# 2x2 average pooling: larger stores, one order of transfers, and each transfer split over two queues

## The chip, the cores and the metric

The kernel runs on one core of a Trainium2 chip. The metric is the device time of the execution in microseconds (us). The profiler gives, for one execution, the span from the first to the last instruction and the work inside it.

## What is computed

The input is a float32 tensor of 32 x 128 planes of 256 x 256 numbers. Each plane is averaged over windows of 2 x 2 that do not overlap, so the output has planes of 128 x 128.

```python
n, c, h, w = 32, 128, 256, 256       # kernel_size = 2, stride = 2
for i in range(h_out):
    for j in range(w_out):
        window = x[:, :, 2*i : 2*i + 2, 2*j : 2*j + 2]
        output[:, :, i, j] = np.mean(window, axis=(2, 3))
```

1073.74 MB are read and 268.44 MB are written.

## The kernel before

Two neighbouring input rows make one output row. The kernel takes such a pair, 512 numbers or 2 KB, as a *unit*; there are 32 x 128 x 128 of them, 4096 for each of the 128 partitions. A *piece* is a number of units per partition that are loaded, worked on and stored together. The units of one partition in a piece lie one behind the other in memory, so a piece of 32 units is a run of 64 KB per partition in the input and a run of 16 KB per partition in the output.

The loop runs over a plan: 126 pieces of 32 units, then two groups of smaller pieces, 16, 8 and 8 units, and 8, 8, 8, 4, 2, 1 and 1 units (lines 58 to 65). For each piece it does five things:

1. The sync queue loads the piece into `in_tile` (line 84). There are two such tiles of 64 KB per partition, so a load waits until the piece two before it has been read.
2. VectorE adds the second row of each pair to the first, in place (line 87; 256 numbers for each unit).
3. VectorE adds each even column to the odd one next to it and writes `col_sum` (line 96; 128 numbers for each unit). There are three such tiles.
4. ScalarE multiplies by 0.25, in place (line 108).
5. ScalarE's queue stores the result (line 110).

Loads and stores are thus two separate streams. All loads are issued by SyncE, all stores by ScalarE, and both run on the same transfer engines at the same time. The framework's scheduler places the waits; the order of the instructions on each engine is that of the loop.

Of the kernel before, what the change touches and what calls it, by code (L numbers as in the profile page):

```python
# [1 line left out]

# [4 lines left out]


@with_exitstack  # L10
def kernel(
    ctx: ExitStack,
    tc: tile.TileContext,
    x: bass.AP,
    kernel_size: bass.AP,
    stride: bass.AP,
    out: bass.AP,
):
    nc = tc.nc
    P = nc.NUM_PARTITIONS  # L20

    n, c, h, w = x.shape
    k = int(kernel_size)
    s = int(stride)
    h_out = (h - k) // s + 1
    w_out = (w - k) // s + 1
    R = n * c * h_out

    if k == s and 2 <= k <= 4 and R > 0 and R % P == 0:
        _nonoverlap_pool(ctx, tc, x, out, k, n, c, h, w, h_out, w_out)  # L30
    else:
        _generic_pool(ctx, tc, x, out, k, s, n, c, h, w, h_out, w_out)


def _nonoverlap_pool(ctx, tc, x, out, k, n, c, h, w, h_out, w_out):
    nc = tc.nc
    P = nc.NUM_PARTITIONS
    s = k
    R = n * c * h_out

    hv = h_out * s
    xs = x if hv == h else x[:, :, 0:hv, :]
    xv = xs.rearrange("n c (ho a) w -> (n c ho) (a w)", a=s)
    ov = out.rearrange("n c ho wo -> (n c ho) wo")
    assert xv.shape == (R, s * w) and ov.shape == (R, w_out)

    wu = w_out * s

    unit_bytes = s * w * 4
    G_MAIN = max(1, min(R // P, (64 * 1024) // unit_bytes))  # L50

    total_units = R // P
    nmain, rem_units = divmod(total_units, G_MAIN)
    plan: list[list[int]] = [[G_MAIN] for _ in range(nmain)]
    if rem_units:
        plan.append([rem_units])

    if G_MAIN % 32 == 0 and nmain >= 4 and rem_units == 0:
        u = G_MAIN // 32
        tail = [  # L60
            [16 * u, 8 * u, 8 * u],
            [8 * u, 8 * u, 8 * u, 4 * u, 2 * u, u, u],
        ]
        assert all(sum(t) == G_MAIN for t in tail)
        plan = plan[:-2] + tail

    sbuf = ctx.enter_context(tc.tile_pool(name="sbuf", bufs=2))

    inv = 1.0 / float(k * k)

    r0 = 0
    for parts in plan:
        in_tile = sbuf.tile([P, G_MAIN, s * w], mybir.dt.float32, name="in_tile")
        g0 = 0
        for g in parts:
            rows = P * g
            xt = xv[r0 : r0 + rows].rearrange("(p g) f -> p g f", p=P)
            ot = ov[r0 : r0 + rows].rearrange("(p g) f -> p g f", p=P)
            r0 += rows

            it = in_tile[:, g0 : g0 + g]
            g0 += g

            nc.sync.dma_start(out=it, in_=xt)

            for di in range(1, k):
                nc.vector.tensor_add(  # L87
                    out=it[:, :, 0:w],
                    in0=it[:, :, 0:w],
                    in1=it[:, :, di * w : (di + 1) * w],  # L90
                )

            col_sum = sbuf.tile(
                [P, G_MAIN, w_out], mybir.dt.float32, name="col_sum", bufs=3
            )
            nc.vector.tensor_add(  # L96
                out=col_sum[:, :g],
                in0=it[:, :, 0:wu:s],
                in1=it[:, :, 1 : wu + 1 : s],
            )  # L100
            for dj in range(2, k):
                nc.vector.tensor_add(
                    out=col_sum[:, :g],
                    in0=col_sum[:, :g],
                    in1=it[:, :, dj : wu + dj : s],
                )

            nc.scalar.mul(out=col_sum[:, :g], in_=col_sum[:, :g], mul=inv)  # L108

            nc.scalar.dma_start(out=ot, in_=col_sum[:, :g])  # L110
        assert g0 <= G_MAIN

    assert r0 == R, (r0, R)


def _generic_pool(ctx, tc, x, out, k, s, n, c, h, w, h_out, w_out):
    nc = tc.nc
    P = nc.NUM_PARTITIONS

    planes = n * c  # L120
    xp = x.rearrange("n c h w -> (n c) h w")
    op = out.rearrange("n c ho wo -> (n c) ho wo")

    if h_out <= 0 or w_out <= 0 or planes == 0:
        return

    max_in_bytes_per_part = 48 * 1024

    def rows_for(bi):
        return (bi - 1) * s + k  # L130

    BI = 1
    while BI < h_out and rows_for(BI + 1) * w * 4 <= max_in_bytes_per_part:
        BI += 1

    inv = 1.0 / float(k * k)

    pool = ctx.enter_context(tc.tile_pool(name="gen", bufs=2))

    for p0 in range(0, planes, P):  # L140
        pn = min(P, planes - p0)
        for i0 in range(0, h_out, BI):
            bi = min(BI, h_out - i0)
            rows_needed = rows_for(bi)

            in_t = pool.tile([P, rows_for(BI), w], mybir.dt.float32, name="g_in")
            nc.sync.dma_start(
                out=in_t[:pn, :rows_needed, :],
                in_=xp[p0 : p0 + pn, i0 * s : i0 * s + rows_needed, :],
            )  # L150

            acc = pool.tile([P, BI, w_out], mybir.dt.float32, name="g_acc")
            first = True
            for di in range(k):
                for dj in range(k):
                    src = in_t[
                        :pn,
                        di : di + (bi - 1) * s + 1 : s,
                        dj : dj + (w_out - 1) * s + 1 : s,
                    ]  # L160
                    if first:
                        nc.vector.tensor_copy(out=acc[:pn, :bi, :], in_=src)
                        first = False
                    else:
                        nc.vector.tensor_add(
                            out=acc[:pn, :bi, :], in0=acc[:pn, :bi, :], in1=src
                        )

            nc.scalar.mul(out=acc[:pn, :bi, :], in_=acc[:pn, :bi, :], mul=inv)

            nc.scalar.dma_start(
                out=op[p0 : p0 + pn, i0 : i0 + bi, :], in_=acc[:pn, :bi, :]
            )


# [1 line left out]
_INS = ['x', 'kernel_size', 'stride']  # L177
_OUTS = [((32, 128, 128, 128), 'float32')]
#: Inputs that are plain numbers.
_NUMBERS = {'kernel_size': 2, 'stride': 2}  # L180


# [26 lines left out]
```

## Time and profile before

| | |
|---|---|
| device time, median of 10 runs | 3106.39 us (3106.22 to 3106.78) |
| device time of the profiled execution | 3106.49 us |
| its span | 3104.7 us |
| row add, 32 units (line 87) | 126 times, 8692 ns each |
| column add, 32 units (line 96) | 126 times, 4425 ns each |
| scale, 32 units (line 108) | 126 times, 3616 ns each |
| store, from issue to landing, median of the full pieces | 31.6 us |
| load, from issue to landing, median of the full pieces | 35.1 us |
| VectorE waits for loads, in total | 1406.7 us |
| ScalarE waits for VectorE, in total | 2635.8 us |

The busy time of an engine is the time in which it works; its idle time costs nothing where another resource sets the end. A load's time from issue to landing contains the time in which it waits for the transfers ahead of it. The queue named q1 carries the loads and q10 the stores. A packet is one contiguous run that one transfer engine moves, or the small write with which the engine reports that its part is done; each transfer has one of these on each of 16 engines.

The beginning and the end of the span, as the timeline shows them: the first load is issued at 0.73 us and VectorE starts on it at 22.65 us. The last full piece reaches VectorE at 3043.20 us. The last store, of one unit, is issued at 3102.36 us and lands 1.5 us later.

### The profile page before, as it was taken

To read this page: it belongs to the slowest core of one execution; us is meant where nothing else is said; L and a number is where in the kernel's file an instruction comes from. 1 tells how busy PE (TensorE), PEld (TensorE's weight loads), DVE (VectorE), ACT (ScalarE), POOL (GpSimd) and SP (SyncE) were. 2 spreads that over 40 slices of the span, in tenths; PEclk is the share of its full clock that TensorE was granted. 3 is DMA by queue.
4 is the path that set the end of the run, shared out by engine and by line. 5 is a ranking of instruction groups with operands and counts; after the bars stand their busy time and mean duration, and the time that the engine had idled before them with its cause. 6 is when DMAs were issued, how large, how long until landed. Compare 5 with 4: busy or idle time off the path is not lost. (4 is left out here: it accounts for less than half of the span.)

```text
span 3104.7 us, 1126 instructions
## 1 busy us (share of the span) xinstructions
DVE 1681.3 (54%) x272; ACT 465.8 (15%) x137; POOL 0.2 (0%) x4
## 2 busy tenths in 40 slices
DVE  4555555555555555555555555555555555555556
ACT  1111111111111111111111111111111111111112
POOL 0000000000000000000000000000000000000000
DMA  9999999999999999999999999999999999999999
GB/s 418 437 439 425 436 439 425 436 438 426 436 439 426 435 439 430 431 439 434 428 438 435 427 438 437 426 437 437 426 437 437 427 435 438 428 435 437 428 435 396
DMA packets 39176, 1342.26 MB, mean 432 GB/s; under 512 B 4352, under 2 KB 4736, under 8 KB 5888
## 3 DMA queue, kind: packets, MB, share of 16 engines
q1 hardware_dynamic: 19584, 1073.75, 79.9%
q10 hardware_dynamic: 19584, 268.44, 20.2%
q14 instruction: 8, 0.07, 0.0%
HBM read 1073.74 MB, written 268.44 MB: 432 GB/s over the span
## 5 line engine op out<-in xcount | busy, mean ns | idle before, releaser
L87 DVE TENSOR_TENSOR in_tile<-in_tile 128x8192 f32<-128x8192 f32 (+4 forms) x136 | 1113.8, 8190 | 1406.8 <-DMA in_tile<-in_x_dram 1406.7
L108 ACT ACTIVATE col_sum<-col_sum 128x4096 f32<-128x4096 f32 (+4 forms) x136 | 464.5, 3415 | 2635.8 <-DVE col_sum L96 2635.8
L96 DVE TENSOR_TENSOR col_sum<-in_tile 128x4096 f32<-128x4096 f32 (+4 forms) x136 | 567.7, 4174 | 14.0 <-DMA out_dram<-col_sum 1.9
L108 ACT ACT_TABLE_LOAD x1 | 1.3, 1283 | 0.7 <-PEq L190 0.7
L190 POOL MEMSET const-bfloat16-1.0<- 128x1 bf16 x1 | 0.1, 101 | 0.0
L190 POOL MEMSET const-uint8-127<- 128x1 uint8 x1 | 0.1, 101 | 0.0
L190 POOL MEMSET const-float32-0.0<- 128x1 f32 x1 | 0.1, 98 | 0.2 <-issue 0.2
L190 POOL MEMSET const-float32-1.0<- 128x1 f32 x1 | 0.1, 98 | 0.0
## 6 DMA issues: line engine op xcount, KB each, us to landing
out_dram<-col_sum ACTq DMA_DIRECT2D x126, 2048.0 KB, 31.6
in_tile<-in_x_dram SPq DMA_DIRECT2D x5, 2048.0 KB, 27.5
in_tile<-in_x_dram SPq DMA_DIRECT2D x1, 4096.0 KB, 25.5
out_dram<-col_sum ACTq DMA_DIRECT2D x5, 512.0 KB, 12.0
in_tile<-in_x_dram SPq DMA_DIRECT2D x126, 35.1
out_dram<-col_sum ACTq DMA_DIRECT2D x1, 1024.0 KB, 12.8
in_tile<-in_x_dram SPq DMA_DIRECT2D x1, 1024.0 KB, 16.2
in_tile<-in_x_dram SPq DMA_DIRECT2D x1, 512.0 KB, 16.8
```

Source lines behind the costliest of these rows:

```text
L87: nc.vector.tensor_add(out=it[:, :, 0:w], in0=it[:, :, 0:w], in1=it[:, :, di * w : (di + 1) * w],)
L96: nc.vector.tensor_add(out=col_sum[:, :g], in0=it[:, :, 0:wu:s], in1=it[:, :, 1 : wu + 1 : s],)
L108: nc.scalar.mul(out=col_sum[:, :g], in_=col_sum[:, :g], mul=inv)
L190: nc = _bacc.Bacc("TRN2", target_bir_lowering=False, num_devices=1)
```

## The change

The changed kernel computes the same thing with the same three operations per piece, and differs in how the data is moved.

- **Groups.** 127 units make a group, loaded in four pieces of 31, 32, 32 and 32 units. There are 32 groups and a rest of 32 units. In memory the rows of a group lie 254 KB apart from partition to partition, and a piece is a run of 62 or 64 KB in it.
- **Stores.** The results of a whole group are collected in `res`, a tile of 158 units per partition, and stored in one transfer with a run of 63.5 KB per partition. Groups use it from unit 0 and from unit 31 in turn, so that the first piece of a group doesn't overlap the results of the group before, while the other pieces do.
- **Order.** The schedule is written by hand. The store of a group is issued after the first load of the next group and before its second load.
- **Split.** Every transfer is issued in two halves: the even partitions on SyncE's queue and the odd partitions on ScalarE's queue. ScalarE's own instructions and its transfers are in one program order.
- **Last piece of a group.** Its column add and scale are done in two steps, all but 8 units and then 8 units.
- **Tail.** The rest is loaded in two halves of 16 units. In ScalarE's program order these loads stand behind the scales of the last group. The last group's store follows them; then the two halves are worked on and stored in one transfer of 16 KB per partition.

```diff
+IN_UNITS = 32
+GROUP = 127
+FIRST = GROUP - 3 * IN_UNITS
+
+def _pool_2x2(ctx, tc, x, out, units):
...
+    in_pool = ctx.enter_context(tc.tile_pool(name="inp", bufs=2))
+    out_pool = ctx.enter_context(tc.tile_pool(name="outp", bufs=1))
+    res = out_pool.tile([P, GROUP + FIRST, w_out], f32, name="res")
...
+    def move(dst, src):
+        nc.sync.dma_start(out=dst[0::2], in_=src[0::2])
+        nc.scalar.dma_start(out=dst[1::2], in_=src[1::2])
+
+    def rows(it):
+        nc.vector.tensor_add(out=it[:, :, 0:w], in0=it[:, :, 0:w], in1=it[:, :, w:])
+
+    def cols(it, dst):
+        nc.vector.tensor_add(out=dst, in0=it[:, :, 0:w:2], in1=it[:, :, 1:w:2])
+
+    def scale(dst):
+        nc.scalar.mul(out=dst, in_=dst, mul=0.25)
+
+    groups, rest = divmod(units - 1, GROUP)
+    rest += 1
...
+    for k in range(groups):
...
+        base = 0 if k % 2 == 0 else FIRST
+        spans = [(FIRST + i * IN_UNITS, IN_UNITS) for i in range(3)]
+        if base == 0:
+            pieces = [(0, FIRST)] + spans
+        else:
+            pieces = [(3 * IN_UNITS, FIRST)] + [(a - FIRST, g) for a, g in spans]
+        jobs += [(xt[:, a : a + g], g, res[:, base + a : base + a + g]) for a, g in pieces]
+        stores.append((ot, res[:, base : base + GROUP]))
+
+    ctx.enter_context(tc.manual_schedule())
...
+    def load(j):
+        if j < len(jobs):
+            src, g, _ = jobs[j]
+            tiles[j] = new_in()[:, :g]
+            move(tiles[j], src)
+
+    load(0)
+    load(1)
+    for j, (_, g, dst) in enumerate(jobs):
+        it = tiles.pop(j)
+        rows(it)
+        if j % 4 < 3:
+            cols(it, dst)
+            load(j + 2)
+            scale(dst)
+        else:
+            for a, b in ((0, g - 8), (g - 8, g)):
+                cols(it[:, a:b], dst[:, a:b])
+                scale(dst[:, a:b])
+            if j + 1 < len(jobs):
+                move(*stores[j // 4])
+                load(j + 2)
...
+    it, tout = new_in(), new_in()
...
+    for a, b in cuts:
+        move(it[:, a:b], xt[:, a:b])
+    move(*stores[-1])
+    for a, b in cuts:
+        rows(it[:, a:b])
+        cols(it[:, a:b], to[:, a:b])
+        scale(to[:, a:b])
+    move(ot, to[:, :rest])
```

The function `_nonoverlap_pool` and its plan are removed. The general path for other sizes stays as it is and isn't used here.

## The prediction

> **What bounds the kernel now.** I read the page's head first, then the slices, then the transfer queues, then windows over single stages, and last the timeline. The page:
>
> ```profile
> span 3104.7 us, 1126 instructions
> DVE 1681.3 (54%) x272; ACT 465.8 (15%) x137; POOL 0.2 (0%) x4
> DMA  9999999999999999999999999999999999999999
> DMA packets 39176, 1342.26 MB, mean 432 GB/s; under 512 B 4352, under 2 KB 4736, under 8 KB 5888
> q1 hardware_dynamic: 19584, 1073.75, 79.9%
> q10 hardware_dynamic: 19584, 268.44, 20.2%
> ```
>
> VectorE is busy for half the span, ScalarE for a seventh; the transfer engines are busy in all 40 slices. Loads (q1) and stores (q10) share their time as 80 to 20, as they share the bytes: a stored byte costs what a loaded one does. So the span is bytes, plus a price per packet, plus the time in which no packet moves. The windows (length, busy time of each engine, clock, transfer share, GB/s) show where the last part lies:
>
> ```profile
> 66.69:3043.20 2976.51, 1613.42 (x247) 444.78 (x123) 0.00 (x0) 1.00 1.00 433
> 3086.00:3098.00 12.00, 8.63 (x7) 2.74 (x3) 0.00 (x0) 1.00 0.96 394
> 3098.00:3104.70 6.70, 2.16 (x6) 1.03 (x3) 0.00 (x0) 1.00 0.33 119
> ```
>
> The first runs from the third to the 126th piece: 123 pieces of 8.389 MB in and 2.097 MB out in 2976.51 us, 24.199 us a piece, 433.3 GB/s, share 1.00. No gap is left there; only the last 7 us are thin. One period of the timeline:
>
> ```profile
> 2994.84 8.69 DVE L87 TENSOR_TENSOR in_tile<-in_tile 128x8192 f32<-128x8192 f32 x1 [10.97 <-DMA in_tile<-in_x_dram]
> 3003.63 4.43 DVE L96 TENSOR_TENSOR col_sum<-in_tile 128x4096 f32<-128x4096 f32 x1
> 3008.08 0.33 SPq L84 DMA_DIRECT2D in_tile<-in_x_dram  x1
> 3008.09 3.62 ACT L108 ACTIVATE col_sum<-col_sum 128x4096 f32<-128x4096 f32 x1 [20.56 <-DVE col_sum L96]
> 3011.73 0.34 ACTq L110 DMA_DIRECT2D out_dram<-col_sum  x1
> ```
>
> VectorE idles 11 us of 24 for the load: compute has room.
>
> [...]
>
> **The price of a packet.** 10.486 MB at 435.2 GB/s are 24.094 us. The other 0.105 us of a piece are spread over 18 packets per engine (8 loads, 8 stores, 2 completion writes): 5.8 ns each. From above, two short windows of the transfer view (packets, MB, share), the first with loads alone, the others the last 6.7 us:
>
> ```profile
> q1 hardware_dynamic: 112, 7.34, 99.6%
> ...
> q10 hardware_dynamic: 650, 0.76, 31.8%
> q1 hardware_dynamic: 20, 0.03, 1.3%
> ```
>
> 112 packets took 99.6% of 16 x 17 us = 270.9 us, their bytes need 269.9: 9 ns each. 670 took 33.1% of 16 x 6.7 = 35.5 us for bytes worth 29.0: 9.6 ns each. I take 5.8, which the loop shows with two queues at work, and keep 9.5 as the other end.
>
> **The change part by part.**
>
> (a) Fewer, larger packets. Before: 39168/16 = 2448 per engine. After: 128 loads plus 2 tail loads, each 8 packets and 2 completion writes per engine, 1300; 33 stores likewise, 330; together 1630. Saved: 818 x 5.8 ns = 4.7 us (7.8 at 9.5 ns).
>
> (b) One order instead of two streams. Four loads, then the store of the group before placed behind the first load of the next. In the loop this costs nothing if the queues never run dry. Usual piece: the next-but-one load is issued 13.2 us after VectorE starts (8.79 + 4.43), while the load between takes 18.7 to 19.3 us: 5 us of cover. Last piece of a group: 8.79, 24 columns units 3.36 (between 2.29 and 4.43 of the two sizes seen), ScalarE on 24 units 2.76 (between 1.91 and 3.62), on 8 units 1.06, hand-overs 0.1: the store is issued at 16.1, and the load behind it on both queues 0.34 later. The 31-unit load in flight covers 18.7. A 64 KB store lands 1.5 us after its issue, 0.15 of it data, so 1.35 us pass before or after the data: about 1.2 us of cover remain. Taken as nothing; without that cover each 0.1 us costs 31 x 0.1 = 3 us. The odd half of every load now stands in ScalarE's queue before a scale and waits for the column add; behind it only that scale waits, which waits for the same add. VectorE's second column add of a group waits for the store that reads this half of `res`; that store is ahead in the same queues of the load that VectorE waits for anyway.
>
> (c) VectorE and ScalarE: 32 further short instructions each, from splitting the last piece; hidden under 11 us of idle per piece.
>
> (d) The end. Start: VectorE's first instruction comes at 22.65, its 8.389 MB are worth 19.28 and 9 packets 0.05, so 3.3 us are fixed. Until the last big load (number 127): 1065.35 MB in and 31 stores of 8.323 MB out, 1323.37 MB, 3040.8 us; 1590 packets, 9.2 us. VectorE starts on it at 3053.3. By then SyncE has issued the even halves of both tail loads (they wait for piece 126 alone), but their odd halves stand in ScalarE's queue behind all scales of piece 127, until 3053.3 + 16.1 = 3069.4. The even halves, 4.19 MB, keep the engines busy for 9.7 us; then nothing can be sent until about 3070.7: **a gap of 7.7 us**. Then the odd tail halves (4.19 MB) and SyncE's even half of the big store (4.16 MB) share the engines. Packets of two queues alternate (a store of before, worth 4.8 us, took 31.6 to land beside a load): four of 1.2 and four of 2.4 us bring the first tail half in at 3085.2, the second by 3090.0. VectorE needs 2 x (4.43 + 2.29) = 13.5 us from 3085.2: 3098.7; ScalarE 1.91: 3100.6. The big store has ended at 3099.6, so there is a second gap of 2.3 us. The last store, 2.097 MB, lands 1.35 + 4.85 us later, 3106.8; before, 0.8 us lay between the last landing (issue 3102.36 plus 1.5) and the end. Span 3107.6.
>
> Against the profiled 3104.7 that is +2.9 us: 4.7 saved in the loop, the rest and 2.9 more given back in the tail, where the kernel before breaks its last two pieces down to one unit and stores each at once. The profiled execution took 3106.49 with its span of 3104.7; the median is 3106.39. I add 2.9 to the median: **3109.3 us**, no change by the bound used here: 0.2% is 6.2 us, 3100.2 to 3112.6, about what a measurement can tell from no change.
>
> **Rivals.**
> 1. Faster. Two queues with equal large packets hide each other's packet price wholly: the loop showed 5.8 ns with two queues, a single queue 9. That would save 1630 x 5.8 ns = 9.5 us more: 3099.8. Against it: the price was still there with two queues always full. The tail gap doesn't close in this case.
> 2. Slower: stores alone are slower than stores among loads. Before, both queues are at work in every slice, so no window shows writes alone; after, some 19 us in every 96 are nothing but writes. Their 268.4 MB are worth 617 us; each per cent less rate costs 6.2 us. It decides from half a per cent (3.3 us beyond my forecast); at 3%, a guess, 3128. For it: nothing but the absence of evidence; against: the equal cost per byte in the page.
> 3. The cover of 1.2 us at the end of each group fails, because a queue that joins late waits longer for its first packet: 1 us short is 31 us, 3140.
> 4. The change doesn't do what it says:[...] loads and stores would take twice as long, about 6200 us.[...]
>
> A load's rows per partition now lie 254 KB apart, not 64. [...]the 64 KB of before ran at full rate. I count a loss there with rival 2.
>
> **How the numbers follow.** Forecast 0.64 (its own range 3104 to 3114), rival 1 0.10, rival 2 0.18, rival 3 0.05, rival 4 0.03. Faster by over 0.2%: most of rival 1 and a sliver of the forecast, 0.08. Slower: rivals 2 to 4 but for small losses, 0.24, plus 0.06 of the forecast, 0.30. Same: 0.62. The range runs from just above rival 1 to within rival 2, 3101 to 3126.
>
> **What would show it.** Packets near 26,080 of the two queues; VectorE's starts on the pieces of a group spaced 38.5 (the store lies between), 19.3, 19.3 and 18.7 us, 95.9 in sum; transfer share 1.00 in any window of the loop; then a stretch near 3063 to 3070 with share 0, a second of 2 us before the last store, and VectorE's first tail add near 3085. A group period of over 96.2 us speaks for rival 2 or 3 (which of them, the window over the store tells); under 95.7, for rival 1. A tail load whose odd half leaves before piece 127 is scaled would prove step (d) wrong.

## The result, and the profile after

| | before | after |
|---|---|---|
| device time, median | 3106.41 us (29 runs) | 3134.29 us (8 runs, 3131.95 to 3138.40) |
| ratio to before | | 1.0089 [1.0081, 1.0098] |
| device time of the profiled execution | 3106.49 us | 3131.95 us |
| its span | 3104.7 us | 3130.2 us |

The changed kernel is 0.9% slower, 25 us more than the forecast of 3109.3 and 8 us above the upper end of the range. The profiled execution is the lowest of the eight, so the sums below explain 3131.95 and leave 2.3 us of the median unexplained.

The page of the changed kernel, head and transfer queues:

```profile
span 3130.2 us, 1398 instructions
DVE 1681.7 (54%) x292; ACT 467.5 (15%) x163; POOL 0.2 (0%) x4
DMA  9999999999999999999999999999999999999998
DMA packets 26090, 1342.28 MB, mean 429 GB/s; under 512 B 5216, under 2 KB 5216, under 8 KB 5216
q10 hardware_dynamic: 13040, 671.10, 50.0%
q1 hardware_dynamic: 13040, 671.10, 49.7%
```

The bytes are the same, the packets are the 2 x 13040 = 26080 that the forecast counted, VectorE is as busy as before, and the transfer engines are busy in every slice. Still the span is 25.5 us longer. The slices cannot show where: a loss of 0.7 us in every 97 does not move a digit. One turn of the loop on the timeline (start, length, engine, line, what it does, and in brackets the idle time before it):

```profile
1047.81 8.69 DVE L69 TENSOR_TENSOR in_tile<-in_tile 128x8192 f32<-128x8192 f32 x1 [6.19 <-DMA in_tile<-in_x_dram]
1056.61 4.49 DVE L72 TENSOR_TENSOR res<-in_tile 128x3072 f32<-128x3072 f32 x2
1060.00 3.71 ACT L75 ACTIVATE res<-res 128x3072 f32<-128x3072 f32 x2 [14.18 <-DVE res L72]
1063.74 0.51 SPq L65 DMA_DIRECT2D out_dram<-res  x1
1064.35 56.36 SPq L65 DMA_DIRECT2D in_tile<-in_x_dram  x3
1066.57 8.42 DVE L69 TENSOR_TENSOR in_tile<-in_tile 128x7936 f32<-128x7936 f32 x1 [5.47 <-DMA in_tile<-in_x_dram]
...
1107.00 8.69 DVE L69 TENSOR_TENSOR in_tile<-in_tile 128x8192 f32<-128x8192 f32 x1 [27.68 <-DMA in_tile<-in_x_dram]
```

The last piece of a group starts at 1047.81 and its store is issued at 1063.74, 15.9 us later (forecast: 16.1). VectorE starts the next piece at 1066.57 and the one behind the store at 1107.00. That is 40.4 us, and a store with a load is worth 38.5. In the mean of 29 groups, the second to the thirtieth, VectorE's starts lie 39.69, 18.63, 19.47 and 18.79 us apart, 96.58 in sum (the *period* below), against 38.5, 19.3, 19.3, 18.7 and 95.9 in the forecast. The excess of 0.68 us in each of 31 groups is 21 us, and VectorE in fact starts on the last piece of the last group at 3074.22, forecast 3053.3.

Windows of the changed kernel (length, busy time of DVE, ACT and POOL, clock, transfer share, GB/s), first before a store, in it and over its end, then three in the tail:

```profile
194.00:197.00 3.00, 0.00 (x0) 0.57 (x1) 0.00 (x0) 1.00 0.92 389
198.00:212.00 14.00, 12.14 (x2) 1.25 (x1) 0.00 (x0) 1.00 1.03 446
210.00:220.00 10.00, 0.17 (x1) 3.51 (x1) 0.00 (x0) 1.00 1.05 418
3083.00:3092.00 9.00, 4.49 (x2) 3.71 (x2) 0.00 (x0) 1.00 0.35 120
3113.00:3123.00 10.00, 7.50 (x3) 3.82 (x2) 0.00 (x0) 1.00 0.53 228
3123.00:3130.20 7.20, 0.00 (x0) 0.00 (x0) 0.00 (x0) 1.00 0.69 291
```

The store itself runs at full rate (446 GB/s at a share of 1.03; a share over 1 is an effect of the window's edges: its 96 packets, six an engine of 2.40 us, are counted whole in 14 us). At its end, from 210 to 220, the share is 1.05 and the rate only 418: packets are under way, and take longer than their bytes are worth. That is one thing that the page's shares hide.

The records of single packets show it directly. They do not name a transfer engine, so they were joined into 16 chains in which each packet begins where the one before it ended, to a few ns; the 20,864 packets with data fall into 16 chains of 1304. Away from the turns a load packet of 64 KB takes 2418 ns and a store packet of 63.5 KB 2399 ns, almost without scatter.

The records of the kernel before hold other sizes too, and give the prices. A packet of 4 bytes (there are 16 for each transfer, the completion writes) takes 9 ns, one of 2 KB 84, of 16 KB 611, of 32 KB 1213 and of 64 KB 2418, in the median. From 2 to 64 KB that is 2334 ns for 62 KB, 27.20 GB/s on an engine and 435.2 on the 16, which is the rate that the forecast reckons with; about 9 ns of each packet are left. In the chains of the changed kernel a packet begins some 4 ns before the one ahead has ended (2414 ns lie between the starts of two load packets of 64 KB), so that about 5 ns of the 9 count.

In the changed kernel, mean time above the usual, by place in the store:

```
store packets 2 to 6 of 8   +1 ns
store packet 7              +4 ns
store packet 8            +422 ns
first load packet behind  +176 ns
```

With the small gaps between them the turn from storing to loading costs 0.614 us on an engine, 31 x 0.614 = 19.0 us, nearly the whole loss of the loop. The other part of the loss is in the tail:

```profile
3074.22 8.69 DVE L69 TENSOR_TENSOR in_tile<-in_tile 128x8192 f32<-128x8192 f32 x1 [6.20 <-DMA in_tile<-in_x_dram]
3083.01 4.49 DVE L72 TENSOR_TENSOR res<-in_tile 128x3072 f32<-128x3072 f32 x2
3086.40 2.76 ACT L75 ACTIVATE res<-res 128x3072 f32<-128x3072 f32 x1 [14.74 <-DVE res L72]
3087.60 1.13 ACTq L66 DMA_DIRECT2D in_tile<-in_x_dram  x2
3089.07 1.04 ACT L75 ACTIVATE res<-res 128x1024 f32<-128x1024 f32 x1
3090.14 0.51 SPq L65 DMA_DIRECT2D out_dram<-res  x1
...
3098.80 4.42 DVE L69 TENSOR_TENSOR in_tile<-in_tile 128x4096 f32<-128x4096 f32 x1 [11.29 <-DMA in_tile<-in_x_dram]
3111.58 2.29 DVE L72 TENSOR_TENSOR in_tile<-in_tile 128x2048 f32<-128x2048 f32 x1 [8.36 <-DMA in_tile<-in_x_dram]
...
3122.50 0.50 SPq L65 DMA_DIRECT2D out_dram<-in_tile  x1
```

The odd tail halves leave on ScalarE's queue only at 3087.60, when the last column add has ended (3083.01 + 4.49), and the window from 3083 shows the hole that this makes: a share of 0.35. From 3074.22 to the end are 56.0 us; the forecast had 54.3.

### The profile page after: what moved, and what is told of

The parts are those of the page before. It is cut to its first block, busy times and chain, and to the rows that moved or that the text cites. A ratio compares the mean times of both kernels' runs of the same rounds, so it can differ in the third digit from the quotient of the medians.

```text
span 3130.2 us, 1398 instructions
## 1 busy us (share of the span) xinstructions
DVE 1681.7 (54%) x292; ACT 467.5 (15%) x163; POOL 0.2 (0%) x4
## 3 DMA queue, kind: packets, MB, share of 16 engines
q10 hardware_dynamic: 13040, 671.10, 50.0%
q1 hardware_dynamic: 13040, 671.10, 49.7%
## 4 chain that ended last, share of the span: by engine, by line
DMA 69%; DVE 26%; ACT 4%; ACTq 1%; issue 0%; DVEq 0%
DMA in_tile<-in_x_dram 69%; DVE in_tile L69 18%; DVE res L72 8%; ACT res L75 4%; ACTq L66 1%; DVE in_tile L72 0%; ACT in_tile L75 0%; DVEq L72 0%; DVEq L69 0%
## 5 line engine op out<-in xcount | busy, mean ns | idle before, releaser
L69 DVE TENSOR_TENSOR in_tile<-in_tile 128x8192 f32<-128x8192 f32 (+2 forms) x130 | 1112.9, 8560 | 1419.3 <-DMA in_tile<-in_x_dram 1419.3
L75 ACT ACTIVATE res<-res 128x4096 f32<-128x4096 f32 (+3 forms) x160 | 462.4, 2909 | 2590.4 <-DVE res L72 2590.4
L72 DVE TENSOR_TENSOR res<-in_tile 128x4096 f32<-128x4096 f32 (+3 forms) x160 | 564.3, 3544 | 11.1 <-DVE in_tile L69 0.9
```

Of the source, the lines that this page charges most:

```text
L69: nc.vector.tensor_add(out=it[:, :, 0:w], in0=it[:, :, 0:w], in1=it[:, :, w:])
L72: nc.vector.tensor_add(out=dst, in0=it[:, :, 0:w:2], in1=it[:, :, 1:w:2])
L75: nc.scalar.mul(out=dst, in_=dst, mul=0.25)
```

## The experiments

Two questions were open: why the turn costs 0.6 us, and what the two queues have to do with it. "Turn" below is the mean time that the last store packet and the first load packet behind it take above their usual time, with the gap between them. The recorded expectations name their theories by letters; the text around them says in words what stood and what fell. All ratios are to the kernel before.

**One queue.**

```diff
-        nc.sync.dma_start(out=dst[0::2], in_=src[0::2])
-        nc.scalar.dma_start(out=dst[1::2], in_=src[1::2])
+        nc.sync.dma_start(out=dst, in_=src)
```

> Every transfer is issued whole on the sync queue, as without the split; the order of loads and stores is that of the changed kernel. Theory A (at the end of each store the engines have nothing else to send until its last writes have landed, about 0.65 us for each of 31 stores): the group period stays near 96.5 us. The tail loads no longer stand behind ScalarE's scales, so the gap of some 8 us at the end closes: about 3125 us. Theory B (the split into even and odd partitions is what costs): the period falls to 95.9 us, with the closed gap about 3104 us. Theory C (stores alone run at a lower rate all along): period 96.5, no difference from A in the loop.

Measured 3116.61 us, ratio 1.0033 [1.0022, 1.0044]; period 96.36 us; turn 0.43 us. The tail of this kernel on the timeline:

```profile
3061.64 0.81 SPq L65 DMA_DIRECT2D in_tile<-in_x_dram  x2
...
3067.73 8.69 DVE L68 TENSOR_TENSOR in_tile<-in_tile 128x8192 f32<-128x8192 f32 x1 [6.13 <-DMA in_tile<-in_x_dram]
...
3080.94 4.42 DVE L68 TENSOR_TENSOR in_tile<-in_tile 128x4096 f32<-128x4096 f32 x1
```

Both tail loads leave at 3061.64, ahead of the last piece, and VectorE needs no wait for the first of them at 3080.94. From 3067.73 to the end (3112.7) are 45.0 us instead of 56.0. So giving ScalarE's queue half of every transfer costs 11.0 us in the tail, close to the gaps of 7.7 and 2.3 us in step (d), and 6.5 us in the loop, which the forecast had not.

**The two halves of a store apart in time.** SyncE's half of the store is issued before the next load and ScalarE's half behind it, so that one queue always loads while the other stores.

```diff
-                move(*stores[j // 4])
-                load(j + 2)
+                ot, rt = stores[j // 4]
+                nc.sync.dma_start(out=ot[0::2], in_=rt[0::2])
+                load(j + 2)
+                nc.scalar.dma_start(out=ot[1::2], in_=rt[1::2])
```

> As the changed kernel, but in the loop ScalarE's half of each store is issued after the next group's second load, so that each half store runs beside a half load of the other queue. Theory A: a load always fills the engines when a store ends, the group period falls from 96.5 to about 95.9 us, 20 us in all: about 3114 us. Theory B (the split costs): no change, about 3134 us. Theory C (stores alone run at a lower rate): also faster, about 3114 us; it is told from A by the rate inside a store of the changed kernel.

Measured 3155.99 us, 1.0161 [1.0140, 1.0182]; period 97.24. The opposite of what was expected: 41 us of stretched packets per engine, 28 of them on the one or two load packets just ahead of a store packet.

**The store in two transfers, on two queues.** The first 64 units, which the last piece doesn't touch, then the other 63.

```diff
-                move(*stores[j // 4])
+                ot, rt = stores[j // 4]
+                move(ot[:, 0:64], rt[:, 0:64])
+                move(ot[:, 64:GROUP], rt[:, 64:GROUP])
```

> As the changed kernel, but each store of the loop is issued as two, of 64 and of 63 units, one behind the other in both queues: twice the store ends, the same number of changes between storing and loading. 320 more packets per engine are worth 2 us. Theory A1 (the wait belongs to the completion write of a store): 13 to 20 us more, about 3152 us. Theory A2 (the wait belongs to the change from storing to loading): about 3136 us.

Measured 3122.25 us, 1.0052 [1.0037, 1.0067]; period 96.22; turn 0.016 us. More completion writes, and the turn is free: that completion writes at a turn cost the time is refuted. In the records a completion write takes 9 ns, and the last packet ahead of it is long in one kernel (422 ns above the usual) and not in the other. The tail keeps its gap here, which is most of what is left.

**Groups of 63 units** (pieces of 31 and 32, twice as many stores of half the size, other tail), on two queues.

```diff
-GROUP = 127
-FIRST = GROUP - 3 * IN_UNITS
+GROUP = 63
+FIRST = GROUP - IN_UNITS
...
```

> As the changed kernel, but with groups of 63 units: two loads and one store of 31.5 KB per partition in each of 65 groups, and a rest of one unit. Twice the changes between loading and storing, the same bytes. Bytes and packets give a group period of 47.6 us. Theory A (a fixed cost at each store): 48.3 us, 21 us more over the loop than the changed kernel; with some 6 us more in the tail, where no half piece is left to send while the last piece is worked on, about 3160 us. Theory C (a cost in proportion to the stored bytes): 47.9 us and about 3142 us.

Measured 3269.74 us, 1.0522 [1.0505, 1.0540]; 49.95 us a group where bytes and packets are worth 47.6. Turn 0.88 us, and about 1.4 us more without any packet ahead of each store. Dearer than both expectations: there are twice as many turns, and each of them, with packets of half the size, costs more than one of the changed kernel.

**The late part first.** As e3, with the two transfers exchanged: units 64 to 126 wait for the last piece, and the rest stands behind them.

> As the store in two (64 and 63 units, 3122 us), but the half that holds the last piece goes first, so that no part of a store can be issued before the last scale; packets, bytes and their number are the same. Theory L (the store is issued just too late; the engines that are done first run dry, all start storing in step and turn back to loading together, and that turn costs): the stretched last store packets come back, group period 96.5 us, about 3133 us. Theory P (a store of 16 packets of 32 KB per engine in place of 8 of 64 KB avoids the cost): group period 96.2 us, about 3122 us.

Measured 3167.98 us, 1.0188 [1.0171, 1.0205]; period 97.70, turn 0.78 us. The same packets as e3 in another order, and the turn costs again. It is half of the 1.48 us by which the period is longer than e3's; longer gaps are a part of the other half (29 us per engine in the whole run, against 12).

**Loads on SyncE's queue, stores on ScalarE's**, each whole, as before the change but with the large stores.

```diff
-        nc.sync.dma_start(out=dst[0::2], in_=src[0::2])
-        nc.scalar.dma_start(out=dst[1::2], in_=src[1::2])
+        nc.sync.dma_start(out=dst, in_=src)
+
+    def store(dst, src):
+        nc.scalar.dma_start(out=dst, in_=src)
...
-                move(*stores[j // 4])
+                store(*stores[j // 4])
...
```

> Groups, pieces and big stores of the changed kernel, but all loads whole on the sync queue and all stores whole on ScalarE's queue, as before the change. Each store then runs beside two loads. Theory S (what costs is that a store has the engines to itself, and the turn back to loading): nothing is lost in the loop, 95.9 us a group; fewer packets than the kernel before and no gap in the tail (the tail loads don't stand behind ScalarE's scales): about 3099 us, faster than both. Theory M (large store packets beside large load packets cost 1.3 us a group, as with the half stores out of phase): 97.2 us a group and about 3140 us.

Measured 3317.20 us, 1.0682 [1.0666, 1.0698]. Both expectations missed by far. The packet records show some 120 us of gaps per engine and 100 us of stretched packets: a load of 32 units takes 50.0 us to land in the median, against 41 for its halves in the changed kernel, and with two input tiles the next load is then issued late too. The kernel before ran its two streams without that loss, with stores of a quarter of the size. Why a single store of this size does so much harm was not followed further.

**One queue and the store in two**, the early part first.

> Every transfer whole on the sync queue, and each store of the loop in two, the half that is ready early first. One queue took 3116.6 us, of which about 0.4 us a group is stretched packets at the turn from storing to loading. Theory L: with the first half issued before the queue runs out, the engines stay out of step and the turn costs nothing: group period 95.9 to 96.0 us, about 3104 us. Theory P: the same, as the packets are the smaller ones too; the run that tells L from P is the one with the late half first. If the turn costs whatever the order: about 3117 us.

Measured 3104.78 us (12 runs), 0.9996 [0.9987, 1.0004]; as expected. Its group on the timeline:

```profile
1036.49 0.33 SPq L65 DMA_DIRECT2D in_tile<-in_x_dram  x1
...
1040.13 18.73 SPq L65 DMA_DIRECT2D out_dram<-res  x2
1042.61 8.69 DVE L68 TENSOR_TENSOR in_tile<-in_tile 128x8192 f32<-128x8192 f32 x1 [6.15 <-DMA in_tile<-in_x_dram]
...
1058.97 15.49 SPq L65 DMA_DIRECT2D in_tile<-in_x_dram  x2
```

The two store transfers (merged in one row, from 1040.13 to 1058.86) are issued on either side of the last piece. Period 96.06, turn 0.028 us. This is the best version found, and it can't be told from the kernel before.

**The store issued earlier.** The last piece in three steps (12, 12 and 8 units), the row add included, on the changed kernel (e10), on e9 (e11) and on one queue with the store in one (e13).

```diff
-        rows(it)
         if j % 4 < 3:
+            rows(it)
...
-            for a, b in ((0, g - 8), (g - 8, g)):
+            for a, b in ((0, 12), (12, 24), (24, g)):
+                rows(it[:, a:b])
```

> As the changed kernel, but the last piece of a group is added and scaled in three steps (12, 12 and 8 units, both adds in each step), so that the store is issued about 1.1 us sooner; transfers and their order are the same. Theory L (the queues run dry before the store, which puts the engines in step, and engines in step lose 0.6 us at the turn back to loading): hardly any dry time and a cheaper turn, group period near 96.0 us, 3114 to 3122 us. If the turn costs the same whatever happens before the store: only the dry time goes, 96.3 us, about 3126 us. If the delay of the store plays no part: 3134 us.

> One queue, each store of the loop in two with the early half first (3104.8 us), and the last piece of a group in three steps as well. The turn from storing to loading costs nothing there by now; what is left over bytes and packets is about 4.6 us, some of it in periods of 96.2 to 96.8 us instead of 95.95. If the second half of the store still runs late at times, these go: 3101 to 3103 us. If not, 3104.8 us as before.

> One queue and whole stores (3116.6 us), with the last piece of a group in three steps. One queue hardly ran dry before its stores, but lost 0.4 us at each turn. Theory L with dryness as the only cause of the step: no change, about 3116 us. If an earlier store frees the turn: 3105 to 3110 us.

Measured 3135.17 us (1.0093 [1.0079, 1.0107]), 3105.74 us (0.9997 [0.9989, 1.0006]) and 3120.02 us (1.0043 [1.0029, 1.0057]). No gain in any of them. Where the turn costs nothing, nothing was to be gained; where it costs, it went on costing 0.50 us (e10) and 0.54 us (e13). Why is answered further down.

**The engines set apart.** As e13, with seven small extra loads at the start on fewer and fewer partitions, meant to keep the 16 engines from reaching the turn together.

```diff
+    xf = x.rearrange("n c h w -> (n c) (h w)")
+    rf = res[:].rearrange("p g f -> p (g f)")
+    for i, k in enumerate((14, 12, 10, 8, 6, 4, 2)):
+        part = slice(2048 * i, 2048 * (i + 1))
+        nc.scalar.dma_start(out=rf[0:k, part], in_=xf[0:k, part])
```

> As the run before it (one queue, whole stores, last piece in three steps), and at the very start seven small loads from ScalarE's queue, of 14, 12, 10, 8, 6, 4 and 2 partitions with 8 KB each, into a part of the result tile that is overwritten later. [...]Theory L (engines that turn from storing to loading within about 1 us of each other lose, engines spread over 2 us don't): the stretched packets at the turn go, 3107 to 3110 us, although there is more to transfer. Theory N (the turn costs each engine by itself, whatever the others do): no gain, 2 us more than the run before it.

Measured 3127.32 us, 1.0068 [1.0054, 1.0082], turn 0.53 us. The engines began the stores 2.6 us apart, and the turn cost as much as before. The comparison with e13 says little, since there they were 2.4 us apart without the extra loads; but e1, with 1.1 us between them, loses less (0.43 us), not more. That engines hinder each other by turning at once is not the cause, or not alone.

**Size or early issue?** Three kernels on one queue. x2 is e9 with the two transfers of a store exchanged, the late part first:

```diff
+                move(ot[:, 64:GROUP], rt[:, 64:GROUP])
+                move(ot[:, 0:64], rt[:, 0:64])
```

> One queue, every store in two parts: first units 64 to 126, which need the last piece, then units 0 to 63, which have long been ready. The packets are those of e9_one_queue_store_in_two (3104.8 us, group period 96.06 us), only their order differs, so that nothing of the store is sent early. Theory Z (size: the last packets of a store cost time if they are large, 63.5 KB, and not if they are about 32 KB): 3103 to 3107 us, period under 96.15. Theory O (order: the turn from storing to loading is free only because the first part of the store is issued early, well before the load in flight ends): the turn costs at least what it costs in e1_one_queue (0.4 us a group), 3115 us or more, period over 96.35.

x5 has a small early part and large last packets:

```diff
+                move(ot[:, 0:16], rt[:, 0:16])
+                move(ot[:, 16:GROUP], rt[:, 16:GROUP])
```

> One queue, every store in two parts: first units 0 to 15 (8 KB per partition), issued early, then units 16 to 126 (55.5 KB per partition). Theory Z (size of the last packets): 55.5 KB is nearly the 63.5 KB of e1_one_queue, so the turn costs some 0.35 us a group: 3112 to 3117 us, with the last store packet of a group 0.2 us or more above its usual duration. Theory O (early issue of a first part): 3103 to 3107 us, the last store packet within 0.08 us of its usual duration.

x6 is e4 on one queue:

> One queue, groups of 63 units (pieces of 31 and 32), the store of a group in one transfer of 31.5 KB per partition, no early part; the rest is one unit, so the tail differs. The bytes and packets of a group are worth 47.6 us. Theory Z (size): the turn is free, since the store's packets are no larger than the halves of e9_one_queue_store_in_two; period 47.6 to 47.75, 3112 to 3124 us. Theory O (early issue): each of 65 turns costs 0.4 us as in e1_one_queue or more; period 48.0 or over, 3138 us or more.

Measured 3117.44 us (1.0035 [1.0023, 1.0046]), 3110.33 us (1.0012 [1.0005, 1.0019]) and 3168.85 us (1.0202 [1.0185, 1.0219]). The last store packet was long by 312 ns in x2, 31 ns in x5 and 581 ns in x6. Small packets at full price, large ones at nearly none: the size is refuted three times. x5's time lies between the two expectations, since its period is 96.26, 0.2 us above that of e9. The turn back to loading explains little of that; the place is the turn before it, where the last packet of the load ahead of the store is 221 ns too long in x5 and 20 ns in e9. Why it is so in x5 stays open.

**Cover.** What e9, e3 and x5 share is that the transfer engines still have work when the late part of the store is issued. For each engine and each turn the records give the time from the issue of the store (its late part, if it is in two) to its first packet there. I call that time the engine's cover. Mean cost of the turn in ns, by cover in us, with the number of cases in brackets (16 engines in 31 turns, 64 in x6; *after* is the changed kernel):

```
            under 1     1-1.4     1.4-1.8    1.8-2.2     2.2-3      3-5      over 5
e1         877 ( 36)  730 ( 87)  412 (186)  197 (141)  262 ( 46)    -        -
x2         947 ( 15)  787 (105)  515 (187)  258 (136)  310 ( 53)    -        -
x5            -          -       362 ( 22)   96 (116)   10 (202)  42 (119)  21 ( 37)
x6         828 (346)  704 (442)  382 (146)  136 ( 19)  194 ( 27)  62 ( 44)    -
e9            -          -          -          -          -         -       29 (496)
after         -       918 (101)  623 (219)  430 (172)  377 (  4)    -        -
```

The kernels lie near one curve: 0.7 to 0.9 us of loss with a cover of 1 to 1.4 us, 0.1 to 0.4 at 2 us, little from 3 us on. Not only the turn as a whole counts, but the single engine's cover: within one and the same turn of e1, an engine with 1 us more of it loses 0.47 us less; between turns the slope is 0.60. The loss isn't paid as a gap before the store; it is paid at the turn. In x2 the late transfer is the first of the two, and its own last packet isn't stretched at all (0 ns); the stretched one (+317 ns) is the last of the part behind it, which had been issued 10.8 us ahead.

If so, more cover should free the turn with no early part at all. Three kernels move the short piece of a group to its end (y0, one queue: 32, 32, 32, 31 units; y1, one queue, groups of 124: 32, 32, 32, 28; y2, the changed kernel with 32, 32, 32, 31):

```diff
-FIRST = GROUP - 3 * IN_UNITS
+FIRST = 32
+SIZES = (32, 32, 31)
...
-        spans = [(FIRST + i * IN_UNITS, IN_UNITS) for i in range(3)]
+        spans = [(FIRST + i * IN_UNITS, SIZES[i]) for i in range(3)]
...
-            pieces = [(3 * IN_UNITS, FIRST)] + [(a - FIRST, g) for a, g in spans]
+            pieces = [(GROUP - FIRST, FIRST)] + [(a - FIRST, g) for a, g in spans]
```

> As e1_one_queue (one queue, a store in one transfer, no part of it early), but a group's pieces are 32, 32, 32 and 31 units instead of 31, 32, 32 and 32: VectorE and ScalarE have one unit less to do before the store is issued, and the load in flight meanwhile is one unit longer, about 0.95 us more cover. Theory K (cover: an engine that begins the store less than about 2 us after its issue pays for that with up to 0.9 us, at the end of the store; the packet records of all runs so far lie on one such curve): 3104 to 3109 us, the last store packet and the first load packet behind it together under 0.15 us above their usual duration, where e1 has 0.40. Theory E (what frees the turn is that a part of the store itself is sent early): 3114 us or more, the two packets 0.3 us or more above it.

> As y0_one_queue_short_last_piece with pieces of 32, 32, 32 and 28 units: about 2.5 us more cover than e1_one_queue. The bytes and packets of a group are worth 93.63 us; the rest is 4 units, so that the tail differs and the time alone says little (3112 to 3132 us). Theory K: group period 93.6 to 93.75, the two packets at the turn together under 0.08 us above their usual duration. Theory E: period 93.95 or more, the two packets 0.3 us or more above it.

> The changed kernel itself, on its two queues, with pieces of 32, 32, 32 and 31 units: one number moved. Theory K: the turn falls from 0.61 us a group to under 0.2 and the gaps before the store go, so 3110 to 3120 us, the tail gap staying; period under 96.2. Theory E: 3128 us or more, period 96.45 or more.

Measured 3119.88 us (1.0043 [1.0028, 1.0058]), 3170.69 us (1.0210 [1.0193, 1.0227]) and 3132.32 us (1.0085 [1.0070, 1.0100]). By the times of y0 and y2 the theory of cover fell: turns of 0.52 and 0.58 us where it expected under 0.15 and 0.2. But the records show that the cover did not come: its median is 1.57 us in y0, against 1.68 in e1. What grew is the distance between the first and the last engine at the start of the store, from 1.1 us in e1 to 2.5 in y0, and from 0.7 in the changed kernel to 2.0 in y2. VectorE starts after the last engine has landed (in the changed kernel 0.70 us after that engine has gone on to the next load, and 1.18 us after the median one), so whatever the others are ahead of it is taken from their cover. The same befell e13: 2.4 us apart and 1.49 us of cover in the median, although its store left 0.9 us sooner after VectorE's start on the last piece. In y0, too, a cover of 1.8 to 2.2 us goes with a loss of 0.25 us and one under 1 us with 0.97, as on the curve. Off it are the engines with 3 to 5 us in y0 and e13 (51 and 49 of 496 cases): they still lost 0.30 and 0.25 us, nearly all of it on the first load packet behind the store; their last store packet took 25 and 1 ns more than usual.

y1 has enough of it, a median of 4.9 us. Its timeline over one group:

```profile
1033.66 7.62 DVE L69 TENSOR_TENSOR in_tile<-in_tile 128x7168 f32<-128x7168 f32 x1 [3.73 <-DMA in_tile<-in_x_dram]
1047.56 0.34 SPq L66 DMA_DIRECT2D out_dram<-res  x1
1054.41 8.69 DVE L69 TENSOR_TENSOR in_tile<-in_tile 128x8192 f32<-128x8192 f32 x1 [9.06 <-DMA in_tile<-in_x_dram]
...
1092.49 8.69 DVE L69 TENSOR_TENSOR in_tile<-in_tile 128x8192 f32<-128x8192 f32 x1 [24.93 <-DMA in_tile<-in_x_dram]
```

From 1054.41 to 1092.49 are 38.1 us, and the store of 8.126 MB with a load of 8.389 MB and 18 packets is worth 38.05 at the forecast's prices: the turn is free, 0.018 us in the mean, with a large store in one transfer and nothing of it early. So cover is enough for a store, and an early part is not needed. But from 1033.66 to 1054.41 are 20.75 us for a load worth 19.33. This load stands behind the short one, which covers its issue for 16.9 us only; its cover is 1.7 us in the median, and it loses: 0.24 us of gap before it, 0.43 us on its first packet and 1.02 us on its last. The loss has moved from a store to a load, with the same mark, a last packet that takes about 1 us longer; the period is 95.44 instead of 93.63, which the expectation missed. This load does not lie on the curve: its engines lost 1.8 us with a cover under 1 us and still 1.7 us with more than 3 us. So the curve holds for the late stores of these runs and is no law for every transfer.

## Why the prediction was wrong

**(a) Packets: right.** 26,080 were forecast and came. A price near 5.8 ns fits y1's store and load above (38.1 us where it makes 38.05) and the 5 ns of the records; whether the 818 saved packets brought exactly 4.7 us can't be separated from the loss in the loop. The pitch of 254 KB, about which the forecast was unsure, cost nothing: a load packet of 64 KB takes 2418 ns before and after.

**(b) Order: the step that failed.** It found the weak place, "about 1.2 us of cover remain", and then put its cost down as "Taken as nothing; without that cover each 0.1 us costs 31 x 0.1 = 3 us". Three things were wrong or missing:

- **The lead was counted from the wrong moment.** The step let the 18.7 us of the load in flight begin when VectorE starts, and so had 18.7 - 16.1 = 2.6 us left at the issue of the store, or 1.2 after its 1.35. In the records of the changed kernel the median engine begins that load 1.18 us before VectorE starts, and even the last engine 0.70 us. At the issue of the store, which came at 15.93 us, 1.63 us are left on the median engine, 0.3 after the 1.35. This lead is the *cover* of the table.
- **The 1.35 us were taken for the limit.** They came from the last store of before, one unit into empty queues, and stood for the time in which a queue runs dry. It hardly ran dry: the gaps ahead of the 31 stores add up to 0.7 us an engine. The loss comes at the turn behind the store, and is there at a lead well above 1.35 us: in the changed kernel 0.62 us at 1.4 to 1.8 and 0.43 at 1.8 to 2.2; on one queue, too, up to 0.31 us are left at 2.2 to 3 (0.01 in x5). Why the knee of the curve lies near 2 us no run shows.
- **It treated the 16 engines as one.** They are 0.7 us apart at the store in the changed kernel, and 2.7 us in e9, where every engine has over 5 us of cover. VectorE starts after the last of them.

The size: 0.614 us a turn where the step had 0, times 31 is 19.0 us; with the gaps ahead of the stores 19.7 of the 20.9 us by which VectorE starts late on the last piece. The remaining 1.2 us are not placed. For a usual piece the step was right in its result: such a load has 5 us of cover in e1 and loses nothing.

**(c) VectorE and ScalarE: right.** The store left 15.9 us after VectorE's start, against 16.1.

**(d) The tail: right that the odd halves come late, wrong about what they wait for, and near in its sum partly by luck.** The engines stand without a packet for 6.1 us from 3083 on and for 3.8 us before the last store, 9.9 together, where the step had 7.7 and 2.3. But the odd halves did not wait for all scales: they left 13.4 us after VectorE's start on the last piece, not 16.1, and 1.5 us before the last scale began at 3089.07. The forecast's own sign, "A tail load whose odd half leaves before piece 127 is scaled would prove step (d) wrong", came true. VectorE then started on the first tail half 24.6 us after its start on the last piece (forecast 31.9), but stood 8.36 us before the column add of that half, until a tail load landed, where the forecast had no wait; why it waits there no run shows. The two errors nearly cancel, and 1.7 us too few are left in the sum.

**The sum.** Forecast span 3107.6; + 20.9 before the last piece, + 1.7 behind it: 3130.2.

**Rivals.** The first (packet price hidden) would have needed a period under 95.7. The second, stores alone slower than stores among loads, is refuted: alone, a store packet of 63.5 KB takes 2399 ns and a load packet of 64 KB 2418, the same time per byte. The third is the one that happened, in another form: the forecast gave it 0.05, less than a third of what it gave to the second, and thought of a late first packet, where the store's last packet is the late one. Its size, 31 us for 1 us, was of the right order. The fourth, half transfers that don't reach all engines alike, is refuted: the 16 chains have 1304 packets with data each, which is four of every transfer of 64 partitions, and a load packet takes the same 2418 ns. The forecast's other test, "A group period of over 96.2 us speaks for rival 2 or 3 (which of them, the window over the store tells)", decided rightly.

**What stays open.** Why the loss of a late start is paid by the last packet before the turn rather than the first of the store; why two queues make the turn dearer than one at the same cover (623 against 412 ns at 1.4 to 1.8 us); why the late load of y1 loses 1.7 us whatever its cover; and what sets the distance between the engines. The curve is a correlation over engines and turns within these runs. What shows that a late issue is the cause are e9 and x2, which send the same packets on one queue in two orders and lose 0.03 and 0.49 us at the turn, and the store of y1, which has more cover without an early part and loses 0.02 us.

## What to carry to other kernels

When the transfer engines are the bound, "the queue never runs dry" is not enough (the gaps ahead of the stores were 0.7 us an engine here, the turns 19.0): ask how long before the first engine gets there each transfer is issued, and count that lead from the engines, not from the instruction that waits for the slowest of them (1.2 us later here). In these runs stores that were issued 3.6 us or more ahead of every engine were free at the turn, and those issued 1 to 2 us ahead were not. What shortens this lead at one place in a period cost up to 1 us there with a store, and 1.7 us with the load of y1, every period, and no slice of the page shows it. In these runs a part of a store that was ready early paid when it was issued early, as its own transfer (3104.78 us in e9 against 3116.61 in e1), and tail loads that stood in a program order behind work that they didn't need cost 11.0 us.

## What the runs showed that was not expected

- A store that an engine begins 1 to 2 us after its issue costs 0.1 to 0.9 us, mostly on the last packet before the turn to loading, with hardly a gap before the store.
- More time for the leading engines did not become cover: the engines drifted apart until it was used up (1.1 to 2.5 us between e1 and y0).
- Large stores on a queue of their own beside loads took 3317.20 us, 6.8% more than the kernel before with its small ones.
- Two halves of a store that overlap loads one after the other (3155.99 us) are worse than both at once (3134.29 us).
